# Moving the diagonal blocks of a chunked delta rule inside SBUF instead of through DRAM

## Chip, cores and metric

The kernel runs on one core of a Trainium2 chip. The metric is device time of one execution in microseconds (us). Three runs of the kernel before gave 1262.1 us as the median (1261.81 to 1263.61).

## What is computed

One layer of a hybrid encoder on a sequence of 2048 rows of 1024 numbers, all in float32: an input projection, a windowed attention in 8 heads, a gated delta rule in 4 heads that is run forward and backward, and an output projection. The change lies in the delta rule. Cut to that:

```python
def gated_delta_rule_chunked(q, k, v, g, beta):          # chunks of 64 in the reference
    ...
    k_beta = k * beta[..., None]
    m = jnp.where(strict, jnp.einsum('bhncd,bhnsd->bhncs', k_beta, k) * decay, 0.0)
    t_inv = lax.linalg.triangular_solve(eye + m, jnp.broadcast_to(eye, m.shape),
                                        left_side=True, lower=True, unit_diagonal=True)
    u = jnp.einsum('bhncs,bhnse->bhnce', t_inv, v * beta[..., None])
    w = jnp.einsum('bhncs,bhnsd->bhncd', t_inv, k_beta * jnp.exp(g)[..., None])
    ...
    def step(state, inp):                                # one chunk after another
        v_new = u_i - w_i @ state
        o = (q_i * exp(g_i)) @ state + a_i @ v_new
        state = state * exp(g_last) + k_dec.T @ v_new
```

So each chunk of each head and direction needs the inverse of a unit triangular matrix, and then the chunks of a head are scanned in order.

## The kernel before

**Stages.** `phase_a` makes the projections, the convolutions and the attention. `phase_b` does the delta rule head by head (h = 0 to 3), with chunks of 128 rows (16 chunks, in four groups `c4` of four), and then the output projection. For each head there are four stages:

- `pre_front(h)` loads keys, queries and values from DRAM, transposes them on TensorE, forms the products `gh`, and multiplies them on VectorE (DVE) with decay and beta into the matrices `ma` (L711): for each direction `d` and group `c4` a tile of 128 partitions x 4 chunks x 2 x 128.
- `solve(h)` inverts the diagonal 32x32 blocks: 2 directions x 16 chunks x 4 quarters = 128 blocks, one per partition, in tiles `L` (matrix) and `X` (inverse) of 128 x 32 x 32. It is a loop of 31 steps of two DVE instructions each (L749 multiplies into `tm`, L753 subtracts from `X`).
- `invert(h)` builds the inverses of the whole 128x128 matrices from the small ones, group by group (`hi`), with five products `pi` on TensorE; the small inverses are laid into the block-diagonal tiles `iv` (L776, on DVE and GpSimd (POOL)) and into `ma` (L793, POOL).
- `scan(h)` walks the 16 chunks in both directions at once: per step `pk` -> `r` (DVE) -> `py` -> `yk` (ScalarE, ACT) -> `po` -> state `S` (DVE).

**The path of the blocks.** A block that lies on 32 partitions of `ma` has to come onto one partition for the solve. Before, this goes through DRAM. L716 writes each `ma` matrix whole (256 KB) into `m_d`, whose rows are padded so that the diagonal blocks lie at a regular stride; L739 and L740 read the blocks back, for one direction into `X` and for the other into `L`; L742 copies `X` transposed into the lower half of `L` on DVE; then GpSimd clears `X` and sets its diagonal (L743, L744). After the last step L754 writes `X` to `x_d`, and `invert` reads eight pieces `xc` back (L765), which DVE turns in 32x32 blocks into `xt` (L766). All these DMAs are issued by SyncE (SP), whose queue is in order.

**Filling work.** `sw_units` has 32 units of the output projection for the attention half (`pcs`, L596 to L598 on TensorE, with `mhs` on ACT, `mls` L591 and `xrs` L599 on DVE, and the loads of `mxs` and `xrs` and the store of `part` on SP). They have no part in the delta rule and stand between its instructions.

**What sets the order.** The program's text does not. `set_order` builds the graph of dependences of all instructions, gives each a cost, plans the five engines forward and backward in turn, and pins the order on each engine (PE, DVE, ACT, POOL, SP) that came out best. A change in one place therefore moves instructions on all engines. Each engine works strictly in that order: an instruction that waits holds up all that stand behind it on its engine. `front(h+1)` and `solve(h+1)` run beside `scan(h)`; `invert(h+1)` follows `solve(h+1)`, and `scan(h+1)` follows `invert(h+1)`.

Of the kernel before, what the change touches and what calls it, by code (L numbers as in the profile page):

```python
# [7 lines left out]
F32 = mybir.dt.float32  # L8
F32R = mybir.dt.float32r
AF = mybir.ActivationFunctionType  # L10
# [5 lines left out]
P = 128  # L16
# [3 lines left out]
NCH = 16  # L20
# [526 lines left out]
def phase_b(ctx, wide, xe, ae, late, tc, t, ident, consts, hp, mix_dn, mix_sw, kq_d, v_d, zdn_d, zsw_d, dp, out):  # L547
    nc = tc.nc
    V, A, G, T = nc.vector, nc.scalar, nc.gpsimd, nc.tensor
# [91 lines left out]
    def pre_front(h):  # L641
# [7 lines left out]
        vs = H["vs"] = {}  # L649
        mp = {}  # L650
        ma = H["ma"] = {}
        m_d = dp.tile([2, NCH, 4 * (32 * P + 32)], F32, tag="m_d", name=f"m_d{h}", bufs=2)
        x_d = dp.tile([2, NCH, P, 32], F32, tag="x_d", name=f"x_d{h}", bufs=2)
        for n, c4 in enumerate(FRONT):
            s4 = slice(4 * c4, 4 * c4 + 4)
            cs = slice(c4 * 512, (c4 + 1) * 512)
# [34 lines left out]
            V.tensor_scalar(ssk[:, s4], ssk[:, s4], EPS, None, ALU.add)  # L691
            G.tensor_tensor(nk[:, s4], ssk[:, s4], pw[:, 0, :4], ALU.pow)  # L692
# [34 lines left out]
        for d in range(2):  # L727
            V.tensor_tensor(ck[:, d], bp[:, d], ekd[:, d, :, h], ALU.mult)

        H["solve"] = m_d, x_d, mp  # L730
        return H

    def solve(h, H):
        m_d, x_d, _ = H["solve"]
        L = qa.tile([P, 32, 32], F32, tag="L", name=f"L{h}")
        X = qa.tile([P, 32, 32], F32, tag="X", name=f"X{h}")
        lv = [m_d[d].rearrange("u (p y) -> (u p) y", p=4)[:, : 32 * P] for d in range(2)]
        lv = [a.rearrange("q (r x) -> q r x", x=P)[:, :, :32] for a in lv]
        dma(X[0:64], lv[0])  # L739
        dma(L[64:128], lv[1])  # L740
        x = X.rearrange("p r c -> p (r c)")
        V.tensor_copy(L[0:64], X[0:64].rearrange("p r c -> p c r"))  # L742
        G.memset(x, 0.0)  # L743
        G.memset(x[:, ::33], 1.0)  # L744
        for c in range(31):
            n = 31 - c
            tm = qa.tile([P, 256], F32, tag="tm", name=f"tm{h}_{c}")
            tv = tm[:, : n * (c + 1)].rearrange("p (r k) -> p r k", k=c + 1)
            V.tensor_tensor(  # L749
                tv, L[:, c + 1 :, c : c + 1].to_broadcast([P, n, c + 1]),  # L750
                X[:, c : c + 1, 0 : c + 1].to_broadcast([P, n, c + 1]), ALU.mult,
            )
            V.tensor_tensor(X[:, c + 1 :, 0 : c + 1], X[:, c + 1 :, 0 : c + 1], tv, ALU.subtract)  # L753
        dma(x_d.rearrange("d u (p r) c -> (d u p) (r c)", p=4), X.rearrange("p r c -> p (r c)"))  # L754

    def invert(h, H):
        _, x_d, mp = H["solve"]
        for hi in range(4):
            e1, p2, e2, e3 = (z[hi % len(z)] for z in zts)
            m = mp[hi]  # L760
# [1 line left out]
            for d, c4 in ((0, hi), (1, 3 - hi)):  # L762
                xc = qb.tile([P, 4, 32], F32, tag="xc", name=f"xc{h}_{d}_{c4}", bufs=4)
                xt = qb.tile([P, 4, 32], F32, tag="xt", name=f"xt{h}_{d}_{c4}", bufs=4)
                dma(xc, x_d[d, 4 * c4 : 4 * c4 + 4].rearrange("u i c -> i u c"))  # L765
                V.transpose(xt.rearrange("p u c -> p (u c)"), xc.rearrange("p u c -> p (u c)"))  # L766
# [97 lines left out]
    def post(h, H, groups):  # L864
        def of(a):
            return a.rearrange("p (g c) -> p g c", c=4)[:, groups[0] : groups[1] + 1 : groups[1] - groups[0]]

        nm = f"{h}_{groups[0]}"
        so = rp.tile([P, 2, 8], F32, tag="so", name=f"sso{nm}")
        for k, c4 in enumerate(groups):  # L870
            for c in range(4):
                jk = rp.tile([P, P], F32, tag="jko", name=f"jko{nm}_{k}_{c}", bufs=3)
# [544 lines left out]
```

## Time and profile before

| | |
|---|---|
| median of three runs | 1262.1 us (1261.81 to 1263.61) |
| the profiled execution, its time | 1270.01 us |
| its span in the profile | 1268.0 us |
| mean granted TensorE clock | 0.989 |
| DVE busy | 953.7 us (75% of the span) |
| ACT busy | 725.8 us (57%) |
| POOL busy | 529.2 us (42%) |

Busy time of an engine is the union of its instructions. A matmul's end is modelled, and matmuls overlap, so TensorE (PE) can be called busy without being at its peak. An idle time is put down to what released the instruction behind it; "<-" reads "was released by". In windows, each engine's busy time in a stretch is followed by its number of instructions; PEclk is the share of TensorE's clock that was granted, DMA the mean busy share of the 16 DMA engines. Rows of DMA issues give the time from issue to landing. In the time of the span, `phase_a` fills about the first 680 us, the delta rule's stages the stretch from there to about 1185, and the output projection of the delta half the rest.

### The profile page before, as it was taken

What the parts mean: (1) busy time and instruction counts of PE and PEld (TensorE: products, weight loads), DVE (VectorE), ACT (ScalarE), POOL (GpSimd) and SP (SyncE); (2) the same over time, 40 slices, a digit from 0 to 9 for tenths busy, and PEclk for the clock granted to TensorE, in tenths of its full rate; (3) what the DMA queues carried; (4) which work ended last, traced back from release to release, by engine and by line L of the source; (5) the groups of instructions that cost most, each with busy time, mean ns of one, the idle gap of its engine ahead of it and who ended that gap; (6) DMA issues with size and microseconds to landing.
All of it is one profiled execution on the core that took longest, in us unless ns stands there. A gap on an engine that the chain in (4) does not pass through costs nothing.

```text
span 1268.0 us, 22351 instructions
## 1 busy us (share of the span) xinstructions
PE 1210.5 (95%) x7018; PEld 1037.4 (82%) x7018; DVE 953.7 (75%) x2320; ACT 725.8 (57%) x2167; POOL 529.2 (42%) x845
## 2 busy tenths in 40 slices
PE   6999999999999999999999998999889899999898
PEld 5998888788889988887777777888789689888776
DVE  4523689999854379999995587698769779876765
ACT  6432476666534367766665438658557845685421
POOL 2243454763302276556422304613742441670541
PEclk9999999999999999999999999999889999999999
DMA  7553243513544434431016848967955875854785
GB/s 259 172 160 125 75 154 100 173 60 102 166 145 125 144 110 137 137 96 55 34 51 207 238 141 245 264 189 207 268 166 174 236 200 152 242 175 122 238 269 199
DMA packets 232294, 206.39 MB, mean 163 GB/s; under 512 B 49137, under 2 KB 181873, under 8 KB 232177
## 3 DMA queue, kind: packets, MB, share of 16 engines
q1 hardware_dynamic: 232176, 204.97, 53.0%
q8 instruction: 56, 0.92, 0.3%
q14 instruction: 62, 0.50, 0.1%
HBM read 139.84 MB, written 65.08 MB: 162 GB/s over the span
## 4 chain that ended last, share of the span: by engine, by line
PE 67%; DVE 13%; DMA 9%; ACT 4%; issue 3%; POOL 1%; SPq 1%; DVEq 0%; ACTq 0%; POOLq 0%
PE pf_c L199 5%; PE pf_c L201 5%; PE pf_c L200 5%; PE pf_z L199 4%; PE pf_z L200 4%; PE pf_z L201 4%; PE pi L781 3%; PE pq_q L212 2%; PE pq_q L211 2%; PE pt L390 2%; PE pq_q L210 2%; DMA xc<-x_d 2%; PE py L830 2%; PE po L839 2%; PE pcs L596 2%
## 5 line engine op out<-in xcount | busy, mean ns | idle before, releaser
L199 PE MATMUL pf_c<-xhi,wh_c 128*128 128x512 f32 x384 | 155.7, 405 | 0.8 <-DVE acc L269 0.8
L200 PE MATMUL pf_c<-xlo,wh_c 128*128 128x512 f32 x384 | 154.7, 403 | 0.0
L201 PE MATMUL pf_c<-xhi,wl_c 128*128 128x512 f32 x384 | 154.3, 402 | 0.0
L269 DVE SCALAR_TENSOR_TENSOR acc<-pf_c,cw,acc 128x512 f32<-128x512 f32 (+1 forms) x192 | 140.8, 742 | 2.6 <-POOL acc L259 0.7
L385 POOL TENSOR_SCALAR pr<-pr,st 128x384 f32<-128x384 f32 (+1 forms) x128 | 79.4, 639 | 98.0 <-DVE st L383 71.2
L394 ACT ACTIVATE ph<-pt 128x512 fp32r<-128x512 f32 x92 | 53.0, 595 | 60.5 <-PE pt L390 51.5
L376 ACT ACTIVATE pr<-pr,st 128x384 f32<-128x384 f32 (+1 forms) x128 | 76.2, 597 | 17.8 <-DVE st L372 17.4
L199 PEld LDWEIGHTS pf_c<-xhi,wh_c 128*128 128x128 f32 x384 | 72.5, 189 | 13.5 <-DVE acc L269 1.3
L201 PEld LDWEIGHTS pf_c<-xhi,wl_c 128*128 128x128 f32 x384 | 72.3, 188 | 12.9
L200 PEld LDWEIGHTS pf_c<-xlo,wh_c 128*128 128x128 f32 x384 | 72.4, 188 | 11.6
L835 ACT ACTIVATE yk<-py,ck 128x128 f32<-128x128 f32 x120 | 43.9, 366 | 62.0 <-PE py L830 61.2
L372 DVE CUSTOM_DVE_ANT_0 pr<-s,mask,sink 128x384 f32<-128x384 f32 (+1 forms) x128 | 73.4, 593 | 2.5 <-PE s L371 1.0
L211 PE MATMUL pq_q<-wh_q,xlo 128*128 128x256 f32 x256 | 72.1, 282 | 0.0
L212 PE MATMUL pq_q<-wl_q,xhi 128*128 128x256 f32 x256 | 71.9, 281 | 0.0
L210 PE MATMUL pq_q<-wh_q,xhi 128*128 128x256 f32 x256 | 71.4, 280 | 0.0
L390 PE MATMUL pt<-ident,pr 128*128 128x128 f32 x368 | 69.5, 274 | 1.8 <-DVE pl L395 1.1
L395 DVE TENSOR_TENSOR pl<-pt,ph 128x512 fp32r<-128x512 f32 x92 | 61.6, 681 | 6.1 <-ACT ph L394 5.6
L390 PEld LDWEIGHTS pt<-ident,pr 128*128 128x128 f32 x368 | 47.8, 140 | 20.4 <-DVE pl L395 4.4
L596 PE MATMUL pcs<-wohs,mhs 128*128 128x512 f32 x128 | 58.3, 456 | 4.4 <-ACT mhs L590 2.7
L692 POOL TENSOR_TENSOR nk<-ssk,pw 128x4 f32<-128x4 f32 x16 | 16.5, 1029 | 106.8 <-DVE ssk L691 106.6
L597 PE MATMUL pcs<-wohs,mls 128*128 128x512 f32 x128 | 56.1, 438 | 1.7 <-DVE mls L591 1.7
L598 PE MATMUL pcs<-wols,mhs 128*128 128x512 f32 x128 | 55.0, 429 | 0.0
(324 smaller groups left out, 4029.4 us busy)
## 6 DMA issues: line engine op xcount, KB each, us to landing
kqc<-kq_d SPq DMA_DIRECT2D x120, 128.0 KB, 3.1
ws_c<-wt SPq DMA_DIRECT2D x48, 256.0 KB, 3.5
xr<-x SPq DMA_DIRECT2D x16, 512.0 KB, 5.3
k_q<-kq_d SPq DMA_DIRECT2D x16, 512.0 KB, 5.6
mxs<-mix_sw SPq DMA_DIRECT2D x32, 256.0 KB, 3.7
xrs<-x SPq DMA_DIRECT2D x32, 256.0 KB, 3.7
part<-xrs SPq DMA_DIRECT2D x32, 256.0 KB, 2.6
xrd<-part SPq DMA_DIRECT2D x32, 256.0 KB, 4.1
```

Of the source, the lines that this page charges most:

```text
L199: T.matmul(ps, hi[:, k, cs], xhi[b][:, k], start=(k == 0), stop=False)
L200: T.matmul(ps, hi[:, k, cs], xlo[b][:, k], start=False, stop=False)
L201: T.matmul(ps, lo[:, k, cs], xhi[b][:, k], start=False, stop=(k == KC - 1))
L210: T.matmul(ps[:, :n], xh, hi[:, k, :n], start=(k == 0), stop=False)
L211: T.matmul(ps[:, :n], xl, hi[:, k, :n], start=False, stop=False)
L212: T.matmul(ps[:, :n], xh, lo[:, k, :n], start=False, stop=(k == KC - 1))
L269: V.scalar_tensor_tensor(av, ps[:, lo:], cw[:, i, k : k + 1], av, ALU.mult, ALU.add)
L372: V.tensor_tensor_reduce(pr[j][:, :n], ps[:, :n], mask[:, lo * P : hi * P], 1.0, sink[:, hh : hh + 1], ALU.add, ALU.min, accum_out=nm[:, j ...
L376: A.activation(pr[j][:, :n], pr[j][:, :n], AF.Exp, bias=nm[:, j : j + 1], scale=-1.0, accum_out=den[:, j : j + 1])
L385: G.tensor_scalar(pr[j][:, :n], pr[j][:, :n], den[:, j : j + 1], 1.0, ALU.mult, ALU.mult)
L390: T.transpose(pt[:, j], pr[j][:, (kb - lo) * P : (kb - lo + 1) * P], ident)
L596: T.matmul(ps, mh[:, k], wh[:, k], start=(k == 0), stop=False)
```

## The change

The blocks no longer leave SBUF. A tile `z` (128 partitions x 8 x 4 x 32) takes the place of `m_d`: each direction and half of the groups owns 32 partitions of it, and for each `ma` matrix four copies, one for each quarter, bring the diagonal blocks there, two on ACT and two on DVE. In `solve`, two 32x32 turns on DVE (64 partitions x 1024 each) make `L` from `z`; the scratch `tm` of the steps now lies in `z`. After the steps, one turn of 128 x 1024 makes `Y` from `X`, in the buffer of `L`. In `invert`, four copies (two on ACT, two on DVE) bring each piece from `Y` to `xt`, and the 32x32 turn, which was there before, now goes from `xt` to `xc`. To make room, the junk outputs `jk` and `jko` of the squares on ACT have one buffer in place of three, and a reserve of 1024 bytes per partition becomes 512.

```diff
-SCRATCH = 1024
+SCRATCH = 512
...
-        m_d = dp.tile([2, NCH, 4 * (32 * P + 32)], F32, tag="m_d", name=f"m_d{h}", bufs=2)
-        x_d = dp.tile([2, NCH, P, 32], F32, tag="x_d", name=f"x_d{h}", bufs=2)
+        z = qa.tile([P, 8, 4, 32], F32, tag="Z", name=f"Z{h}")
...
-                    jk = q1.tile([P, P], F32, tag="jk", name=f"jk{h}_{c4}_{j}_{c}", bufs=3)
+                    jk = q1.tile([P, P], F32, tag="jk", name=f"jk{h}_{c4}_{j}_{c}", bufs=1)
...
             for d in range(2):
-                dma(m_d[d, s4, : P * P].rearrange("u (i j) -> i u j", j=P), ma[d, c4][:, :, 0])
+                b = 32 * (2 * d + c4 // 2)
+                for p, q in enumerate(quads):
+                    a = z[b : b + 32, 4 * (c4 % 2) : 4 * (c4 % 2) + 4, p]
+                    if "VAVA"[p] == "A":
+                        A.activation(a, ma[d, c4][q, :, 0, q], AF.Copy)
+                    else:
+                        V.tensor_copy(a, ma[d, c4][q, :, 0, q])
...
     def solve(h, H):
-        m_d, x_d, _ = H["solve"]
+        z = H["solve"][0].rearrange("p u q j -> p j (u q)")
...
-        dma(X[0:64], lv[0])
-        dma(L[64:128], lv[1])
         x = X.rearrange("p r c -> p (r c)")
-        V.tensor_copy(L[0:64], X[0:64].rearrange("p r c -> p c r"))
         G.memset(x, 0.0)
         G.memset(x[:, ::33], 1.0)
+        V.transpose(L[0:64], z[0:64])
+        V.transpose(L[64:128].rearrange("p a b -> p b a"), z[64:128])
+        tm = H["solve"][0].rearrange("p u q j -> p (u q j)")[:, :256]
         for c in range(31):
...
-        dma(x_d.rearrange("d u (p r) c -> (d u p) (r c)", p=4), X.rearrange("p r c -> p (r c)"))
+        Y = H["Y"] = qa.tile([P, 8, 4, 32], F32, tag="L", name=f"Y{h}")
+        V.transpose(Y.rearrange("p u q r -> p r (u q)"), X)
...
-                dma(xc, x_d[d, 4 * c4 : 4 * c4 + 4].rearrange("u i c -> i u c"))
-                V.transpose(xt.rearrange("p u c -> p (u c)"), xc.rearrange("p u c -> p (u c)"))
+                b = 32 * (2 * d + c4 // 2)
+                for p, q in enumerate(quads):
+                    a = Y[b : b + 32, 4 * (c4 % 2) : 4 * (c4 % 2) + 4, p]
+                    if "VAVA"[p] == "A":
+                        A.activation(xt[q], a, AF.Copy)
+                    else:
+                        V.tensor_copy(xt[q], a)
+                V.transpose(xc.rearrange("p u c -> p (u c)"), xt.rearrange("p u c -> p (u c)"))
```

Because the planner sees new instructions, the order moves on every engine. Two places on DVE matter for the prediction. A row is line, operation, output<-inputs with the program's names, and shape; line numbers behind the change are shifted by up to nine.

The first place is where the solve of head 1 begins, beside the scan of head 0 (`r0_0_4` is step 4 of direction 0 of head 0). Before:

```order
L823 SCALAR_TENSOR_TENSOR r0_1_3_9197<-pk0_1_3_9195,negc_4920,vs0_3_8017 128x128
L591 TENSOR_TENSOR mls2_0_10138<-mxs2_0_10135,mhs2_0_10137 128x512
L842 SCALAR_TENSOR_TENSOR S0_0_3_9188<-S0_0_2_9148,egt_4922,po0_0_3_9180 128x128
L856 TENSOR_TENSOR oacc0_3_9091<-po0_1_2_9160,oacc0_3_9091 128x128
L742 COPY L1_10275<-X1_10276 64x1024
L823 SCALAR_TENSOR_TENSOR r0_0_4_9217<-pk0_0_4_9215,negc_4920,vs0_1_7827 128x128
L856 TENSOR_TENSOR oacc0_0_9078<-po0_0_3_9180,oacc0_0_9078 128x128
L842 SCALAR_TENSOR_TENSOR S0_1_3_9208<-S0_1_2_9168,egt_4922,po0_1_3_9200 128x128
L823 SCALAR_TENSOR_TENSOR r0_1_4_9238<-pk0_1_4_9236,negc_4920,vs0_2_7890 128x128
L749 TENSOR_TENSOR tm1_0_10282<-L1_10275,X1_10276 128x31
```

With the change:

```order
L851 SCALAR_TENSOR_TENSOR S0_1_1_9144<-S0_1_0_9104,egt_4922,po0_1_1_9136 128x128
L832 SCALAR_TENSOR_TENSOR r0_0_2_9153<-pk0_0_2_9151,negc_4920,vs0_0_7971 128x128
L865 TENSOR_TENSOR oacc0_0_9094<-po0_0_1_9116,oacc0_0_9094 128x128
L745 STREAM_TRANSPOSE L1_10314<-Z1_9798 64x1024
L775 STREAM_TRANSPOSE xc0_1_1_8926<-xt0_1_1_8927 128x128
L746 STREAM_TRANSPOSE L1_10314<-Z1_9798 64x32x32
L865 TENSOR_TENSOR oacc0_3_9107<-po0_1_1_9136,oacc0_3_9107 128x128
L751 TENSOR_TENSOR Z1_9798<-L1_10314,X1_10315 128x31
```

The first step of the solve has moved from behind step 4 of the scan to behind its step 2, and two turns stand where one copy stood.

The second place is where the same solve ends. Before (the last step is the row with `tm1_30` on its right):

```order
L749 TENSOR_TENSOR tm1_30_10372<-L1_10275,X1_10276 128x31
L694 TENSOR_TENSOR bp2_11356<-beta_4894,ssk2_11354 128x2x4
L842 SCALAR_TENSOR_TENSOR S0_0_14_9676<-S0_0_13_9636,egt_4922,po0_0_14_9668 128x128
L753 TENSOR_TENSOR X1_10276<-X1_10276,tm1_30_10372 128x31
L711 SCALAR_TENSOR_TENSOR ma2_0_11512<-gh2_0_0_11548,bp2_11356,v2_q_7736 128x2x128
L823 SCALAR_TENSOR_TENSOR r0_0_15_9705<-pk0_0_15_9703,negc_4920,vs0_3_8017 128x128
```

With the change:

```order
L755 TENSOR_TENSOR X1_10315<-X1_10315,Z1_9798 128x31
L710 SCALAR_TENSOR_TENSOR ma2_2_11399<-gh2_1_1_11443,bp2_11388,v2_q_7736 128x2x128
L851 SCALAR_TENSOR_TENSOR S0_0_11_9526<-S0_0_10_9486,egt_4922,po0_0_11_9518 128x128
L710 SCALAR_TENSOR_TENSOR ma2_1_11396<-gh2_1_1_11443,bp2_11388,v2_q_7736 128x2x128
L710 SCALAR_TENSOR_TENSOR ma2_2_11399<-gh2_1_1_11443,bp2_11388,v2_q_7736 128x2x128
L721 COPY Z2_11391<-ma2_1_11396 32x4x32
L832 SCALAR_TENSOR_TENSOR r0_0_12_9555<-pk0_0_12_9553,negc_4920,vs0_3_8040 128x128
L867 SCALAR_TENSOR_TENSOR oacc0_2_9268<-po0_0_11_9518,egc_4924,oacc0_2_9268 128x128
L757 STREAM_TRANSPOSE Y1_10382<-X1_10315 128x32x32
L868 TENSOR_TENSOR oacc0_2_9268<-po0_0_11_9518,oacc0_2_9268 128x128
L721 COPY Z2_11391<-ma2_1_11396 32x4x32
L774 COPY xt1_0_0_10385<-Y1_10382 32x128
```

The solve's end has moved from just ahead of the scan's last step (15) to ahead of step 12, and the turn into `Y`, the copies into `xt` and the first copies into `z` for head 2 stand among the scan's steps.

More of the change, by code (lines that the diff above doesn't have):

```diff
@@ L728, in pre_front @@
             V.tensor_tensor(ck[:, d], bp[:, d], ekd[:, d, :, h], ALU.mult)
-        H["solve"] = m_d, x_d, mp
+        H["solve"] = z, mp
         return H
     def solve(h, H):
-        m_d, x_d, _ = H["solve"]
+        z = H["solve"][0].rearrange("p u q j -> p j (u q)")
         L = qa.tile([P, 32, 32], F32, tag="L", name=f"L{h}")
         X = qa.tile([P, 32, 32], F32, tag="X", name=f"X{h}")
-        lv = [m_d[d].rearrange("u (p y) -> (u p) y", p=4)[:, : 32 * P] for d in range(2)]
-        lv = [a.rearrange("q (r x) -> q r x", x=P)[:, :, :32] for a in lv]
-        dma(X[0:64], lv[0])
-        dma(L[64:128], lv[1])
         x = X.rearrange("p r c -> p (r c)")
-        V.tensor_copy(L[0:64], X[0:64].rearrange("p r c -> p c r"))
         G.memset(x, 0.0)
         G.memset(x[:, ::33], 1.0)
+        V.transpose(L[0:64], z[0:64])
+        V.transpose(L[64:128].rearrange("p a b -> p b a"), z[64:128])
+        tm = H["solve"][0].rearrange("p u q j -> p (u q j)")[:, :256]
         for c in range(31):
             n = 31 - c
-            tm = qa.tile([P, 256], F32, tag="tm", name=f"tm{h}_{c}")
             tv = tm[:, : n * (c + 1)].rearrange("p (r k) -> p r k", k=c + 1)
@@ L753, in solve @@
             V.tensor_tensor(X[:, c + 1 :, 0 : c + 1], X[:, c + 1 :, 0 : c + 1], tv, ALU.subtract)
-        dma(x_d.rearrange("d u (p r) c -> (d u p) (r c)", p=4), X.rearrange("p r c -> p (r c)"))
+        Y = H["Y"] = qa.tile([P, 8, 4, 32], F32, tag="L", name=f"Y{h}")
+        V.transpose(Y.rearrange("p u q r -> p r (u q)"), X)
     def invert(h, H):
-        _, x_d, mp = H["solve"]
+        Y, mp = H["Y"], H["solve"][1]
         for hi in range(4):
@@ L871, in post @@
             for c in range(4):
[L872 removed]
+                jk = rp.tile([P, P], F32, tag="jko", name=f"jko{nm}_{k}_{c}", bufs=1)
                 A.activation(jk, H["oacc"][c4][:, c], AF.Square, accum_out=so[:, 0, 4 * k + c : 4 * k + c + 1])
```

## The prediction

> **What bounds the kernel now.** I read the page first: how busy each engine is, and the granted clock.
>
> ```profile
> span 1268.0 us, 22351 instructions
> PE 1210.5 (95%) x7018; PEld 1037.4 (82%) x7018; DVE 953.7 (75%) x2320; ACT 725.8 (57%) x2167; POOL 529.2 (42%) x845
> ```
>
> TensorE is busy for all but 57 us, so a change that takes nothing from it can at best win what it idles, plus what it loses to a lowered clock. Where is that? The windows answer, cut at the stages (each solve runs between two hand-overs, from one head's matrices and inverses to the next scan):
>
> ```profile
> core 0: us, PE busy (x) PEld busy (x) DVE busy (x) ACT busy (x) POOL busy (x), PEclk, DMA share, GB/s
> 40.00:680.00 640.00, 635.80 (x3527) 539.85 (x3526) 494.83 (x1050) 361.95 (x857) 289.90 (x453) 1.00 0.37 116
> 768.00:1115.00 347.00, 317.98 (x2109) 282.53 (x2107) 281.11 (x860) 228.80 (x873) 153.58 (x272) 0.97 0.74 214
> 768.00:823.00 55.00, 48.88 (x306) 42.37 (x305) 38.15 (x105) 40.74 (x149) 34.25 (x67) 0.97 0.95 272
> 823.00:882.00 59.00, 56.53 (x394) 50.49 (x393) 53.04 (x177) 40.88 (x168) 14.22 (x14) 1.00 0.67 197
> 882.00:934.00 52.00, 42.03 (x266) 37.13 (x264) 36.59 (x105) 32.55 (x125) 29.22 (x55) 0.93 0.87 241
> 934.00:990.00 56.00, 55.47 (x380) 50.71 (x381) 50.44 (x161) 38.82 (x157) 19.38 (x27) 0.95 0.59 179
> 990.00:1034.00 44.00, 37.09 (x225) 31.32 (x223) 31.72 (x95) 27.33 (x110) 22.77 (x50) 0.96 0.83 228
> 1034.00:1077.00 43.00, 42.37 (x294) 39.06 (x294) 39.01 (x129) 22.47 (x72) 7.97 (x18) 0.96 0.50 151
> 1077.00:1115.00 38.00, 35.62 (x253) 31.44 (x251) 32.16 (x94) 26.00 (x97) 25.76 (x43) 1.00 0.77 223
> ```
>
> The projections and the attention (40 to 680) leave TensorE idle for 4.2 us in 640: nothing to win there, however the planner shuffles them. The stretch 768 to 1115 has 29.0 us idle, of which the four hand-overs hold 25.4 (6.1, 10.0, 6.9, 2.4). The clock falls there too, and just behind: 1.7 us of full clock are lost in the first hand-over (0.03 of 55), then 3.6, 2.8, 1.8 and 1.7 in the next four rows. In the three solve windows (823, 934, 1034) TensorE is full and DVE is at 142.5 of 158 us, 90%. In the hand-overs DMA is at 0.77 to 0.95, and DVE idles for 50.4 us.
>
> What ends last in a hand-over? The chain of waits between 882 and 934, the waits of the same stretch, and the DMA queue's timeline:
>
> ```profile
> 882.43 6.82 DMA x_d<-X
> 889.27 4.05 DMA xc<-x_d
> ...
> 896.11 2.06 PE pi L781 x8
> ...
> 924.46 6.88 DMA xrs<-x
> 931.41 0.69 DVE xrs L599
> ```
>
> ```profile
> DVE xrs L599 <- DMA xrs<-x: 4.2, 1, 4.2
> PE pi L781 <- DVE iv L776: 3.6, 1, 3.6
> ```
>
> ```profile
> 914.49 3.90 SPq L740 DMA_DIRECT2D L<-m_d  x1
> 918.45 2.28 SPq L819 DMA_DIRECT2D kqc<-kq_d  x2
> ...
> 924.46 0.38 SPq L593 DMA_DIRECT2D xrs<-x  x1
> ```
>
> Two things are to be seen. After the solve, `x_d` and `xc` take 10.9 us before the first product `pi`, and TensorE waits 3.6 us for what they bring. And the issue of `L` holds SyncE's queue for 3.9 us; the queue is in order, so `xrs` of the filling unit is issued at 924.5 and lands at 931.3; DVE stands 4.2 us at L599 with the scan's state update behind it, and TensorE behind that:
>
> ```profile
> PE pk L821 <- DVE S L842: 3.8, 4, 3.2
> L740 SPq DMA_DIRECT2D L<-m_d x4: 597/3568/4602, 726.1 to 1021.9; - x4
> ```
>
> **The change, part by part.** Removed per head: eight writes `m_d`, `X`, `L`, `x_d`, eight reads `xc` (19 DMAs, 76 in all, from SyncE's queue), and the copy L742.
>
> ```profile
> m_d<-ma SPq DMA_DIRECT2D x20, 256.0 KB, 5.6
> x_d<-X SPq DMA_DIRECT2D x4, 512.0 KB, 6.4
> xc<-x_d SPq DMA_DIRECT2D x32, 64.0 KB, 4.0
> L<-m_d SPq DMA_DIRECT2D x4, 256.0 KB, 6.9
> L742 DVE COPY L<-X x4: 1096/1114/1120, 729.8 to 1026.6; 64x1024 f32<-64x1024 f32 x4
> ```
>
> That is 5.6 + 6.9 + 1.1 = 13.6 us of latency ahead of a solve and 6.4 + 4.0 = 10.4 behind it. Not all of it costs time, since the order puts a scan and filling work beside it. What it does cost, by the rows above: the 3.6 us of `pi`, the 3.8 of `pk`, and the lowered clock from 882 to 1077, which follows those idle times (3.6 + 2.8 + 1.8 + 1.7 = 9.9). I add 2 for the other hand-overs, where DVE also waits for `xc` (8.3 us in all, by the row of `xt` waits below). **Waits removed: 19 us.** Bounds: 7.4 if only the two waits go, 37 if all idle and all lost clock of the hand-overs go (25.4 + 11.6).
>
> Added per head on DVE: 16 copies into `z`, 16 into `xt`, two turns of 64x1024 and one of 128x1024. The nearest rows:
>
> ```profile
> L776 DVE COPY iv<-xc x48: 171/218/1206, 779.7 to 1110.2; 32x128 f32<-32x128 f32 x48
> L776 DVE COPY iv<-xt x48: 216/235/1303, 782.7 to 1110.6; 32x128 f32<-32x128 f32 x48
> L776 DVE COPY iv<-xt 32x128 f32<-32x128 f32 x48 | 15.6, 328 | 1.0
> L766 DVE STREAM_TRANSPOSE xt<-xc 128x128 f32<-128x128 f32 x32 | 9.4, 303 | 8.7 <-DMA xc<-x_d 8.3
> ```
>
> A copy of 32x128 takes 0.17 to 0.33 us (the least, and a mean that includes those held to 1.3); I take 0.25, near the medians. A turn of 1024 a partition is not in the trace. From below it costs what L742 does, 1.1 us; from above eight turns of 128, 2.4. I take 1.3, because the turn of 128 at 0.30 is near a plain DVE instruction of that size and a copy's 1.1 grows from there by little. So 32 x 0.25 + 3 x 1.3 - 1.1 = 10.8 us a head (bounds 7.7 and 16.7). [...]
>
> Between 768 and 1115 lie three heads' `z` copies and turns into `L` (3 x (4.0 + 1.5)) and four heads' `Y` and `xt` (4 x (1.3 + 4.0)): 37.7 us. DVE then has 281.1 + 37.7 = 318.8 us of work in that stretch, as much as TensorE (318.0 busy). **Here lies the price**: were the 19 us to go whole, the stretch would be 328 us and DVE 97% busy. It does reach that, but for 20 us at a time:
>
> ```profile
> 960.00:980.00 20.00, 20.00 (x150) 18.62 (x148) 19.60 (x65) 15.32 (x69) 3.82 (x3) 1.00 0.53 161
> 1040.00:1060.00 20.00, 20.00 (x148) 18.66 (x147) 19.35 (x62) 11.34 (x35) 0.00 (x0) 1.00 0.51 157
> ```
>
> Over a whole solve it is 90%, with TensorE as the bound. I take the middle of 90 and 97, 93.5%: 318.8 / 0.935 = 341 us for the stretch. **So DVE gives back 13 of the 19.**
>
> Added on ACT: 32 copies a head.
>
> ```profile
> L799 ACT ACTIVATE ma<-pi x40: 249/268/270, 790.5 to 1149.9; 32x128 f32<-32x128 f32 x40
> ```
>
> At 0.268 that is 8.6 us a head, 34 in all. ACT is idle in the hand-overs for 62 us of 189, which hides it; without that cover it costs what it takes. Before 768 head 0's copies and turns (5.5 us on DVE) lie beside the last gates, where TensorE is full: nothing. One buffer for `jk` and `jko` makes each square wait for its forerunner's end on ACT itself; the planner puts other ACT work between, and I cost it at nothing, with 34 us of the idle taken and 28 left as cover. `z` has one buffer and holds the solve's scratch: copies for head 2 cannot start before the solve of head 1 has ended, and on DVE the rest of `ma` would be late behind them; the order shows the first such copy five rows behind the solve's last step, so this too is nothing. TensorE gets no instruction.
>
> **The sum.** -19 + 13 = -6 us. In the profiled execution that is 1270.0 to 1264 (span 1268 to 1262); it was 7.9 us above the median, so against the median 1262.1 the forecast is **1256 us**. A difference under 0.2%, 2.5 us, cannot be told from no change.
>
> **Rivals.** (1) *DVE becomes the bound, and the kernel slower.* The place is the same stretch. If DVE stays at the 90% of the solve windows, it needs 318.8 / 0.90 = 354 us, 7 more than now: 1269 us; with the upper prices of copy and turn (16.7 a head, some 57 us in the stretch) 376, or 1291. It decides from 92% on: 318.8 / 347. For it speaks that the copies stand in front of scan steps in the order (the second place); against it that the 90% are what TensorE, full there, leaves to DVE. (2) *The waits go and DVE finds room*: 97%, the full 19 us: 1243 us. For it: 50.4 us of DVE idle in the hand-overs, and the solve ends earlier, at step 12 of the scan. (3) *The transfers were hidden anyway*: the scan's chain ends the hand-over, other loads (`xrs`, `kqc`) still land late, and what was won in one queue is waited for in the next: 1262 us. For it: the waits of TensorE in a hand-over are many and short, with other names. [...] Of the same copy some take 1.2 to 1.3 us against a median of 0.22, while GpSimd copies beside them stretch too:
>
> ```profile
> L776 POOL COPY iv<-xt x48: 281/292/808, 789.7 to 1133.8; 32x128 f32<-32x128 f32 x48
> ```
>
> If every added copy is charged the mean, 0.32, the 112 copies of the stretch are 8 us more work: 327 / 0.935 = 349, or 1264 us. [...]
>
> **Chances.** Forecast (1251 to 1262 us) 0.42; rival 1 0.28; rival 2 0.16; rival 3 0.09; rival 4 0.05. Faster by over 0.2%: 0.33 of the forecast, rival 2, and 0.01 of rival 3, in all 0.50. Within 0.2%: 0.07 + 0.01 + 0.06 + 0.02 = 0.16. Slower: 0.02 + 0.27 + 0.02 + 0.03 = 0.34. The range, 1238 to 1276, takes in rival 2 with half its spread (a gain of 24) and rival 1 with half the way to its upper prices; about 0.18 lies outside. The forecast's own range is 1251 (DVE at 95%) to 1262 (92%).
>
> **What would show it.** Right: no wait for `xc`, no issue of 3 us and more on SyncE in the hand-overs, `pi` of head 1 following the solve's last step by some 5 us (a turn, two copies, a turn) and not 14; PEclk above 0.97 from 882 on; DVE over 92% busy between the first inverse and the last. The turn's row gives its price, the copies' rows theirs. Wrong: a span of the stretch over 347 us with DVE above 90% (rival 1), DVE idle in the hand-overs as now (rival 3), or copies with a mean over 0.3 (rival 4).

## The result and the profile after

| | before | after |
|---|---|---|
| median of three runs | 1262.1 us | 1300.08 us (1296.17 to 1300.3) |
| the profiled execution, its span | 1268.0 us | 1298.5 us |
| mean granted TensorE clock | 0.989 | 0.989 |

The kernel became slower by 38 us: the ratio is 1.0288, with a 95% interval of 1.0256 to 1.032. The prediction was 1256 us with a range up to 1276; both the sign and the range were wrong. The two profiled spans lie 30.5 us apart, so the profiles below account for that much of the loss.

The page of the kernel after, engines and three lines of the 40 slices:

```profile
PE 1218.4 (94%) x7018; PEld 1037.0 (80%) x7018; DVE 1021.8 (79%) x2456; ACT 778.9 (60%) x2295; POOL 535.2 (41%) x845
DVE  4523689999754289999985789899999999976775
ACT  5432466755633367666666756768957875786421
DMA  7554242522552444322015736555656444663785
```

TensorE has the same 7018 products. DVE is busy 68 us longer, ACT 53, and DMA is no longer high between slices 24 and 36. Where did TensorE lose the time? The windows of the kernel before, cut at 680, at the end of the first solve and at the end of the last (columns as in the prediction):

```profile
0.00:680.00 680.00, 664.42 (x3711) 566.66 (x3712) 511.47 (x1079) 384.64 (x906) 301.72 (x485) 1.00 0.39 126
680.00:768.00 88.00, 85.25 (x403) 68.83 (x402) 58.18 (x162) 43.32 (x171) 14.09 (x13) 1.00 0.63 179
768.00:1077.00 309.00, 282.37 (x1859) 251.09 (x1857) 248.95 (x766) 202.80 (x777) 127.82 (x229) 0.96 0.74 212
1077.00:1268.00 191.00, 178.42 (x1052) 150.81 (x1050) 135.12 (x314) 95.01 (x316) 85.52 (x118) 1.00 0.67 207
```

The same four stages after, then the three hand-overs (last step of one solve to first step of the next), and at last the stretch of which the prediction spoke, from the first inverse on:

```profile
0.00:680.00 680.00, 659.28 (x3673) 561.53 (x3674) 504.94 (x1045) 376.52 (x878) 302.22 (x479) 1.00 0.39 122
680.00:788.00 108.00, 101.93 (x485) 81.60 (x484) 79.96 (x220) 67.12 (x233) 19.26 (x21) 0.98 0.56 161
788.00:1100.00 312.00, 274.44 (x1801) 240.63 (x1800) 291.63 (x862) 233.16 (x853) 125.18 (x226) 0.97 0.54 166
1100.00:1298.50 198.50, 182.79 (x1065) 153.20 (x1063) 145.25 (x332) 102.14 (x332) 88.56 (x119) 1.00 0.63 199
...
788.00:838.00 50.00, 36.27 (x207) 29.61 (x205) 43.74 (x111) 41.78 (x145) 27.05 (x54) 0.90 0.61 190
890.00:945.00 55.00, 44.96 (x282) 37.27 (x280) 53.03 (x155) 50.90 (x198) 26.46 (x46) 1.00 0.62 192
992.00:1059.00 67.00, 57.92 (x359) 49.54 (x357) 62.68 (x183) 57.82 (x226) 25.67 (x49) 0.95 0.51 156
...
788.00:1137.00 349.00, 307.39 (x2033) 269.53 (x2032) 326.29 (x964) 260.42 (x947) 147.72 (x270) 0.97 0.55 167
```

TensorE's idle time is a window's length less its busy time. Up to the end of the first solve it went from 18.3 to 26.8 us, between the first solve and the last from 26.6 to 37.6, and behind it from 12.6 to 15.7: 22.6 us more in all; the other 7.9 us of the span lie in TensorE's busy time, and why the same products keep it busy longer is not shown. Of the idle time, 5.1 us came up before 680 (15.6 to 20.7), where no added instruction has run yet: there only the order has changed. In the three hand-overs DVE is now busy for 159.5 of 172 us (93%) and ACT for 150.5 (88%). Before, there was room: DVE idled for 50.4 us of the four.

The wait of 3.6 us that TensorE had for `iv` is gone. Others took its place; four of the longest from 788 to 1137 (us in all, times, longest):

```profile
PE gh L701 <- DVE xhi_h L710: 4.6, 2, 2.9
PE py L839 <- DVE r L832: 3.4, 7, 0.8
PE tr L681 <- ACT ks L684: 3.3, 1, 3.3
PE po L841 <- DVE zt L899: 2.8, 2, 2.2
```

All rows of this view added up, DVE ended 24.9 us of TensorE's waits and ACT 13.0; in the same view of before (768 to 1115) it was 17.5 and 9.1.

DVE's timeline behind the solve of head 1 shows what took the place of the transfers (start, us, line, operation; before, the chain had `x_d` and `xc` here, 10.9 us):

```profile
890.71 0.17 DVE L755 TENSOR_TENSOR X<-X,Z 128x31 f32<-128x31 f32 x1
890.80 0.47 DVE L710 SCALAR_TENSOR_TENSOR ma<-gh,bp,v_q 128x256 f32<-128x256 f32 x1
891.20 0.33 DVE L851 SCALAR_TENSOR_TENSOR S<-S,egt,po 128x128 f32<-128x128 f32 x1
891.46 0.86 DVE L710 SCALAR_TENSOR_TENSOR ma<-gh,bp,v_q 128x256 f32<-128x256 f32 x2
...
892.89 1.95 DVE L757 STREAM_TRANSPOSE Y<-X 128x1024 f32<-128x1024 f32 x1
...
895.00 0.93 DVE L721 COPY Z<-ma 32x128 f32<-32x128 f32 x1
895.96 0.22 DVE L774 COPY xt<-Y 32x128 f32<-32x128 f32 x1
...
897.19 0.22 DVE L774 COPY xt<-Y 32x128 f32<-32x128 f32 x1
...
899.59 1.06 DVE L774 COPY xt<-Y 32x128 f32<-32x128 f32 x1
...
901.00 0.88 DVE L774 COPY xt<-Y 32x128 f32<-32x128 f32 x1
```

The first row is the solve's last step. Between it, `Y` and the copies into `xt` stand products for the `ma` of the next head, the scan's `r`, `S` and `oacc`, and copies into `z`; DVE goes from one to the next without a rest, and two of the four `xt` copies take 1.06 and 0.88 us. POOL's timeline has these two rows (the second is two instructions):

```profile
894.91 0.95 POOL L743 MEMSET X<- 128x1024 f32 x1 [5.15 <-DVE Y L757]
899.30 2.49 POOL L672 TENSOR_TENSOR v_q<-v_q,dmask 128x512 f32<-128x512 f32 x2
```

The three long copies each run beside one of these instructions and end less than 0.1 us behind it. It is so in the whole trace: 15 of the 128 added DVE copies took over 0.4 us, and every one of them ended 0.07 to 0.09 us behind an instruction of POOL beside it, while the median copy took 0.22. Such long copies are what the fourth rival charged, with every added copy at the mean of 0.32 us (1264 us); what the 15 took above the median comes to 12 us of DVE over the four heads. That POOL's instructions hold them is not shown: 46 of the other 113 copies also had one beside them, and no run takes POOL's work away.

PE's timeline has the first `pi` of this inverse at 911.17 us, 20.3 us behind the end of the last step; before it was 14.1 (882.0 to 896.11). TensorE did not idle for it this time; the planner had put other products ahead of it:

```profile
911.17 0.39 PE L790 MATMUL pi<-iv,g 128*128 128x128 f32 x2
```

The new rows among the groups by line (busy us, mean ns):

```profile
L774 DVE COPY xt<-Y 32x128 f32<-32x128 f32 x64 | 21.3, 332 | 1.4
L772 ACT ACTIVATE xt<-Y 32x128 f32<-32x128 f32 x64 | 19.7, 307 | 2.3 <-DVE Y L757 1.0
L721 DVE COPY Z<-ma 32x128 f32<-32x128 f32 x40 | 11.8, 295 | 0.7
L746 DVE STREAM_TRANSPOSE L<-Z 64x1024 f32<-64x1024 f32 x4 | 8.4, 2105 | 0.1
L745 DVE STREAM_TRANSPOSE L<-Z 64x1024 f32<-64x1024 f32 x4 | 8.1, 2032 | 0.0
L757 DVE STREAM_TRANSPOSE Y<-X 128x1024 f32<-128x1024 f32 x4 | 7.9, 1967 | 0.0
```

### The profile page after: what moved, and what is told of

It reads as the page before. It is cut to its first block, busy times and chain, and to the rows that moved or that the text cites. A ratio compares the mean times of both kernels' runs of the same rounds, so it can differ in the third digit from the quotient of the medians.

```text
span 1298.5 us, 22500 instructions
## 1 busy us (share of the span) xinstructions
PE 1218.4 (94%) x7018; PEld 1037.0 (80%) x7018; DVE 1021.8 (79%) x2456; ACT 778.9 (60%) x2295; POOL 535.2 (41%) x845
## 4 chain that ended last, share of the span: by engine, by line
PE 58%; DVE 19%; ACT 8%; DMA 7%; issue 4%; POOL 3%; SPq 1%; DVEq 0%; POOLq 0%; ACTq 0%
PE pf_c L201 4%; PE pf_c L200 4%; PE pf_c L199 4%; PE pf_z L199 3%; PE pf_z L201 3%; PE pf_z L200 3%; DVE acc L269 3%; PE pi L790 3%; PE pq_q L212 2%; PE pq_q L211 2%; PE pq_q L210 2%; DMA zs<-wt 2%; PE pt L390 2%; PE py L839 2%; PE po L848 2%
## 5 line engine op out<-in xcount | busy, mean ns | idle before, releaser
L691 POOL TENSOR_TENSOR nk<-ssk,pw 128x4 f32<-128x4 f32 x16 | 16.7, 1045 | 109.3 <-DVE ssk L690 104.1
L190 ACT ACTIVATE wh_c<-ws_c 128x512 fp32r<-128x512 f32 x48 | 30.2, 629 | 50.4 <-DMA ws_c<-wt 20.3
L596 PE MATMUL pcs<-wohs,mhs 128*128 128x512 f32 x128 | 55.7, 435 | 1.8 <-ACT mhs L590 0.6
```

## The experiments

Eighteen kernels were run. Times are medians, ratios are to runs of the kernel before on the same chip (its median lay between 1261.4 and 1264.7 us). They ask four things: what is the order worth by itself, what the single junk buffer, what the copies, what the planner's price of a turn.

### What a new order costs, with nothing else changed

The kernel before, with one constant of the planner moved. Not one instruction differs, only the order.

```diff
-LAG = {"PE": 205, "DVE": 140, "Activation": 160, "Pool": 120, "SP": 2400}
+LAG = {"PE": 205, "DVE": 140, "Activation": 160, "Pool": 120, "SP": 2390}   # e5_nudge_sp
+LAG = {"PE": 206, "DVE": 140, "Activation": 160, "Pool": 120, "SP": 2400}   # e6_nudge_pe
+LAG = {"PE": 205, "DVE": 141, "Activation": 160, "Pool": 120, "SP": 2400}   # e18_nudge_dve
```

> The kernel before, with one of the planner's constants nudged (the lag of a DMA 2390 in place of 2400 ns): same instructions, another order. Theory D (the kernel before stands on an order that came out well, and any edit that makes the planner plan anew loses 10 to 20 us): 1270 to 1285 us. Theory C (the junk buffer's own waits cost what e1 lost): 1262 us within 4.

> The kernel before, with another constant nudged (the lag of TensorE 206 in place of 205 ns): a second draw of the order. Theory D: 1270 to 1285 us, not the same as e5. Theory C: 1262 us within 4.

> The kernel before with the lag that the planner reckons for DVE at 141 in place of 140 ns; no instruction added or removed. Two such nudges gave 1270.9 and 1274.7 us, and the order planned for one junk buffer 1282.6 with the buffers unchanged. Theory A (the order of the kernel before is a chosen one, and any other plan loses 7 to 20 us): 1268 to 1283 us. Theory B (the losses of the earlier plans are chance, as many draws lie at or below 1262): 1255 to 1265 us.

Measured: 1270.89 us, ratio 1.0056 (1.0032 to 1.008); 1274.74, 1.0085 (1.0065 to 1.0105); 1274.46, 1.0105 (1.0064 to 1.0145). All three lose, by 7 to 13 us (their ratios, of 1262). A fourth order of the same instructions, e13 below, loses 20. So the order of the kernel before is a good one among those that the planner draws, and each of the four other draws gave that up. Against the three nudged ones the change lost some 25 to 30 us, against e13 18, not 38.

### The single junk buffer

In the kernel before: one buffer for `jk` and `jko` (and the reserve of 512 bytes); the same with the planner told that there are three, so that the order stays that of before; and the reverse, three buffers with the planner told that there is one. In the changed kernel: three buffers, in bf16 so that they fit.

```diff
-  jk = q1.tile([P, P], F32, tag="jk", ..., bufs=3)     # and jko
+  jk = q1.tile([P, P], F32, tag="jk", ..., bufs=1)     # e1, e7
...
+  bufs = 3 if tag.startswith("jk") else m.bufs         # in set_order: e7
+  bufs = 1 if tag.startswith("jk") else m.bufs         # in set_order: e13, with bufs=3 above
...
-  jk = q1.tile([P, P], F32, tag="jk", ..., bufs=1)     # after
+  jk = q1.tile([P, P], mybir.dt.bfloat16, tag="jk", ..., bufs=3)   # e8
```

> The kernel before, with the junk tiles jk and jko in one buffer and the reserve of 512 bytes; the blocks still go through DRAM. Theory A (the added DVE work is what costs): nothing of it is here, 1262 us, within 3. Theory B (the planner prices the turns and copies too low and leaves too little slack): also 1262, give or take what another order does, some 3 us. Theory C (the single junk buffer makes the squares on ACT wait for each other and draws out the front stage): 1275 to 1295 us, with longer fronts, most of the loss.

> The kernel before with jk and jko in one buffer, while the planner is told three: the order on every engine is that of the kernel before, so only the waits between the squares on ACT are new. Theory C: 1275 to 1285 us, as e1 (1282). Theory D: 1262 to 1266, and the 20 us of e1 come from the order.

> The kernel before with its three junk buffers, but with the planner told that there is one (and 512 bytes more room), so that the order is that of the kernel with one junk buffer (1282.2 us), without the waits for a single buffer. Theory A (waits and order add: 8 us of waits by the run that kept the old order, 10 to 12 of order as in the two nudged plans): 1271 to 1276 us. Theory B (the waits are all of it, the order is free): 1262 to 1265. Theory C (the order is all of it): 1280 to 1283.

> The changed kernel with three buffers for jk and jko again, in bfloat16 so that they fit (the junk is never read). Theory C: 20 of the 38 us come back, 1280 us or lower. Theory D: another draw of the order, anything from 1280 to 1305. Theory A: 1300 as the changed kernel.

Measured: e1 1282.17 us, ratio 1.0163 (1.0139 to 1.0187); e7 1272.69, 1.0061 (1.004 to 1.0081); e13 1282.55, 1.0163 (1.014 to 1.0186); e8 1291.73, 1.022 (1.0191 to 1.0248).

e7 is the clean run: the order is kept, and the single buffer costs 8 us, between what Theory C and Theory D had. The page shows how; it is of the longest execution, 1281.4 us, where the other four took 1272.0 to 1272.7. Its row of engines:

```profile
PE 1214.7 (95%) x7018; PEld 1038.9 (81%) x7018; DVE 956.9 (75%) x2320; ACT 741.4 (58%) x2167; POOL 532.1 (42%) x845
```

ACT is busy for 741.4 us with the same 2167 instructions, against 725.8. The durations of ACT's instructions, added up, are the same (871.8 and 871.2 us); what has grown is their union. With three buffers 175 of the 192 squares begin before the instruction ahead of them on ACT has ended, with one 34 do: 15.6 us, 0.08 us for each square. The waits of DVE from 680 to 1185 show it arriving, first before, then in e7:

```profile
DVE ssk L691 <- ACT jk L690: 8.6, 6, 4.9
DVE ma L711 <- ACT jko L873: 0.9, 1, 0.9
```

```profile
DVE ssk L691 <- ACT jk L690: 12.2, 9, 5.8
DVE ma L711 <- ACT jko L873: 2.2, 1, 2.2
DVE sso L876 <- ACT jko L873: 1.7, 3, 0.8
```

e13 corrects this for another order: with the order that the planner draws for one buffer, three buffers and one take the same time (1282.6 and 1282.2), so there the waits cost nothing and the order all of the 20 us (ACT is busy for 736.9 us in e1 and 729.3 in e13, a growth of half the size). Theory C of e13 held, and the sum "waits and order" that e1 had suggested fell. In the changed kernel, three buffers gain 8 us (1300.1 to 1291.7, intervals apart), though with a new order too; the 20 us of Theory C of e8 did not come.

### Each half alone

e2 is the change with `x_d` and `xc` as before, so only the way from the matrices to the solve lies in SBUF (with one junk buffer). e3 is the kernel before with only the way from the solve to the inverse in SBUF (three junk buffers).

```diff
+  dma(x_d.rearrange("d u (p r) c -> (d u p) (r c)", p=4), X.rearrange("p r c -> p (r c)"))   # e2, in place of Y
+  dma(xc, x_d[d, 4 * c4 : 4 * c4 + 4].rearrange("u i c -> i u c"))                             # e2, in place of the xt copies
...
+  V.transpose(Y.rearrange("p u q r -> p r (u q)"), X)                                          # e3, in place of x_d; xt copies as in the change
```

> The changed kernel, but only the matrices go to the solve inside SBUF; from the solve to the inverse the blocks go through DRAM as before. Of the 68 us that DVE is longer busy with the change, the copies into z and the turns into L less the removed copy are 32, the rest 29. Theory A: loss in proportion, 38 x 32 / 68 = 18, so 1280 us. Theory B: the two turns of 2.05 us that the planner takes for 1.13 are on the path to the solve here, 1275 to 1285. Theory C: the junk buffer is here, so 1285 to 1300.

> The kernel before, but the solve's result goes to the inverse inside SBUF (one turn, copies into xt); the matrices go to the solve through DRAM; junk tiles with three buffers. DVE gets 29 of the 68 us. Theory A: 38 x 29 / 68 = 16, so 1278 us. Theory B: one underpriced turn a head, 1265 to 1275. Theory C: no loss, or the gain of the removed x_d and xc waits, 1250 to 1262.

Measured: 1278.68 us, ratio 1.0139 (1.0119 to 1.0159); 1274.72, 1.0107 (1.008 to 1.0135). The second half alone takes as long as a nudged plan of the kernel before: beyond the lost order nothing is seen of it. The first half alone lies 4 to 8 us over those draws, about what its single junk buffer can cost. The two losses, 16 and 12 us, do not reach 38: both halves together cost more than their sum. That would follow if both fill the same engines; with a new order in each run it is not shown.

### The copies

In the change: all copies on ACT (e4). In e8, the change with three junk buffers: DVE's half on POOL (e9), every copy as a DMA from SBUF to SBUF (e11), every copy twice (e14), one copy of four (e16; three quarters of `z` and `xt` are cleared on POOL in their place, so those diagonal blocks are left out of what is computed).

```diff
-  if "VAVA"[p] == "A":
+  if "AAAA"[p] == "A":                          # e4
...
-  V.tensor_copy(a, ma[d, c4][q, :, 0, q])       # and V.tensor_copy(xt[q], a)
+  G.tensor_copy(a, ma[d, c4][q, :, 0, q])       # e9
...
+  dma(a, ma[d, c4][q, :, 0, q])                 # e11, for all four, and dma(xt[q], a)
...
   V.tensor_copy(a, ma[d, c4][q, :, 0, q])
+  V.tensor_copy(a, ma[d, c4][q, :, 0, q])       # e14, the same for ACT's and for xt
...
+  if p == 0:                                    # e16
       V.tensor_copy(xt[q], a)
+  else:
+      G.memset(xt[q], 0.0)
```

> The changed kernel with all copies on ACT (32 a head more there, some 39 us in all) and none on DVE (41 us less); the turns stay. Theory A: DVE is left with 27 of the 68 us, so 1262 + 38 x 27 / 68 = 1277 us or lower, unless ACT becomes the bound. Theory B: the turns are still underpriced, 1290 to 1300. Theory C: ACT is loaded further, 1300 or more.

> As e8 (three junk buffers), with the copies that were on DVE on GpSimd: 41 us less on DVE, about 37 more on POOL, ACT as in e8. Theory E (in the hand-overs DVE and ACT are both filled by the copies and turns, DVE 93 to 95%, ACT 85 to 89%, so that shifting work between them, as e4 did, wins nothing): DVE falls to some 80% there and the time to 1275 to 1283 us. Theory B (underpriced turns): 1288 to 1295, as e8. Theory D alone (order luck): no direction, 1280 to 1300.

> As e8, with all 64 copies a head made by DMA from SBUF to SBUF, so that DVE and ACT have only the turns to do more than in the kernel before (24 us less 4 for the copy that went). One DMA leg stands where two were, and the matrices are not written out whole. Theory E: the hand-overs are free of the copies, 1265 to 1278 us, the level of the nudged kernels (1271 and 1275) or better. Theory B: 1285 to 1295, the turns are as before. If it is the wait for DMAs that set the hand-overs, also better than e8 only in part, 1280 to 1290.

> The change with three junk buffers (1291.7 us), each copy between quarters made twice (128 more on DVE, 128 more on ACT; the second writes the same as the first, so the result is the same). Theory A (DVE and ACT are full in the hand-overs, so an added copy costs its time there): about 128 x 0.32 = 41 us more on DVE, of which three quarters lie in the stretch of the hand-overs: 15 to 35 us slower, 1307 to 1327 us. Theory B (the copies fit into idle time and the loss is of the order alone): within 8 us, 1284 to 1300 us.

> The change with three junk buffers (1291.7 us) with one copy of four left: of each matrix and of each piece only the first quarter is copied, on DVE; the other quarters of z and xt are cleared on POOL instead, so three of four diagonal blocks are left out of what is computed, while the turns, the solve and all products stay. It takes 128 copies from ACT and 64 from DVE. Theory A (an added copy costs its time: 256 copies more cost 30 us when every one was made twice, so 192 fewer give back 20 to 25): 1265 to 1275 us. Theory B (the second set of copies cost because the first had used up the idle time; the first was mostly hidden): 1280 to 1292 us.

| | us | ratio (95%) | DVE, ACT in the three hand-overs | TensorE's idle in them |
|---|---|---|---|---|
| e4, all on ACT | 1297.81 | 1.0285 (1.0259 to 1.031) | 76%, 93% | 32.0 of 185 us |
| e8, as in the change | 1291.73 | 1.022 (1.0191 to 1.0248) | 94%, 87% | 32.5 of 163 |
| e9, DVE's on POOL | 1282.96 | 1.0159 (1.0108 to 1.021) | 85%, 86% | 25.4 of 146 |
| e11, by DMA | 1328.03 | 1.0518 (1.0477 to 1.056) | - | - |
| e14, twice | 1321.94 | 1.0474 (1.0455 to 1.0493) | 93%, 86% | 46.3 of 198 |
| e16, one of four | 1273.8 | 1.0098 (1.0064 to 1.0132) | 94%, 74% | 20.0 of 136 |

The hand-overs of e14 and of e16, from which two rows of the table come (the others the same way, each cut at its own solves):

```profile
788.00:845.00 57.00, 39.48 (x181) 29.83 (x180) 53.62 (x142) 47.46 (x164) 21.69 (x41) 0.85 0.56 180
891.00:965.00 74.00, 58.91 (x346) 48.57 (x345) 67.94 (x199) 64.23 (x250) 37.35 (x62) 0.93 0.54 169
1017.00:1084.00 67.00, 53.36 (x290) 42.63 (x291) 61.66 (x187) 57.63 (x218) 23.14 (x47) 0.92 0.45 139
```

```profile
778.00:820.00 42.00, 34.91 (x211) 28.72 (x210) 39.01 (x93) 28.36 (x102) 30.00 (x78) 1.00 0.72 224
875.00:921.00 46.00, 38.25 (x257) 32.95 (x256) 42.52 (x129) 34.77 (x150) 27.69 (x62) 1.00 0.66 190
981.00:1029.00 48.00, 42.82 (x272) 35.99 (x270) 46.29 (x137) 37.63 (x163) 28.93 (x66) 1.00 0.57 176
```

With the copies doubled the share of DVE and ACT stays where it was, and the hand-overs grow by 35 us: the engines were full, so an added copy costs most of its time. DVE is busy for 37.7 us more than in e8 and ACT for 41.4, and the kernel takes 30 us longer. It is the same from the other side: three of four copies less take 18.9 us from DVE and 38.1 from ACT, and give back 18 us. The 30 us stand clear of what a draw of the order cost anywhere here (20), the 18 only of the three nudges. Theory A of e14 held, and that of e16 (near the upper end of its range). Which engine makes the copies matters less: on ACT alone the fill moves from DVE (76%) to ACT (93%), and nothing is gained (Theory A of e4, 1277 us, failed); on POOL, which had the most idle time, DVE's half costs 9 us less, which a draw of the order can nearly explain by itself (6 us, e15 below).

The DMAs were the worst, beyond every theory of e11 (1265 to 1295 us). SyncE issues 256 of them, and each holds its queue for 0.6 us, 159 us in all; POOL and DVE wait for what they bring. The source view of the pieces `xt` in e11: SyncE's issues of them, and who waited for them (us, times):

```profile
L768 SPq DMA_DIRECT2D xt<-Y x128: 585/599/1612, 789.8 to 1185.0; - x128
...
  POOL iv L779: 26.6, 6
  DVE xc L769: 13.0, 7
```

### The planner's price of a turn, and both remedies together

The planner had priced a turn by the rule for other DVE instructions. e10 gives it the measured one; e12 adds e9's copies on POOL; e17 is e12 with SyncE's lag at 2390, and e15 is e8 with that lag.

```diff
+            if "ranspose" in str(i.opcode):
+                return 62 + 1.94 * m        # e10, e12, e17
...
+    G.tensor_copy(xt[q], a)                 # e12, e17, in place of V; z's copies too
...
-LAG = {... "SP": 2400}
+LAG = {... "SP": 2390}                      # e15, e17
```

> As e8, with the planner's price of a 32x32 turn set to what the profile shows (62 ns + 1.94 ns an element: 2.05 us for 1024 a partition in place of 1.14). Theory B: the planner leaves the room, 1272 to 1282 us. Theory E: the work is still there, 1287 to 1296. Theory D: anything within 8 of 1292.

> The change with three junk buffers, with DVE's half of the copies on POOL, and with the planner told the measured price of a turn (62 ns + 1.94 ns for each element of a partition). Alone, the first of these two brought 1291.7 to 1283.0, the second to 1284.2. Theory A (what is left over the kernel before is DVE's and ACT's fill, part of it ordered by a wrong price): the gains add in part, 1274 to 1279 us, and TensorE's stall in the hand-overs falls below the 42 us of the POOL version. Theory B (both gains are luck of the order and say nothing of copies and turns): the two don't add, 1280 to 1288 us.

> The change with three junk buffers and one constant of the planner moved (the lag that it reckons for SyncE, 2400 to 2390 ns), as in the nudge of the kernel before that cost 7 us. Theory A (the order of the changed kernel is one draw from a scatter of some us, and 1291.7 no unlucky one): 1285 to 1297 us. Theory B (the order of the changed kernel is an unlucky draw by itself, and most of the loss is that): one other draw falls to 1270 to 1280 us.

> The change with three junk buffers, DVE's half of the copies on POOL and the measured price of a turn in the planner (1279.3 us), with the planner's lag for SyncE at 2390 in place of 2400. Theory A (what is left over the kernel before is partly the scatter that any new plan shows, 3 to 8 us either way): 1272 to 1286 us, above 1262 either way. Theory B (the change made well is worth its 19 us of waits, and only the order hides it): a draw below 1262 us.

Measured: e10 1284.22 us, ratio 1.0173 (1.0132 to 1.0213), between Theory B and Theory E and inside Theory D; e12 1279.27, 1.0138 (1.0117 to 1.0159); e15 1285.34, 1.0195 (1.0165 to 1.0225); e17 1273.8, 1.0097 (1.0064 to 1.013). The two remedies add in part, 12 us of 16 (at the upper end of Theory A of e12), and one more draw takes 5.5 us away. e15 shows what a draw alone is worth in the changed kernel, 6 us; by that measure POOL alone (9 us) and the price alone (7.5) are not shown one by one. Both together gain 12.5 us at one lag (e8 to e12) and 11.5 at the other (e15 to e17), which two pairs of draws make likely.

The hand-overs of e17:

```profile
772.00:815.00 43.00, 33.19 (x193) 27.39 (x192) 34.16 (x80) 37.26 (x131) 30.18 (x79) 0.96 0.73 222
871.00:921.00 50.00, 42.91 (x278) 36.17 (x277) 41.99 (x114) 47.05 (x188) 35.16 (x78) 1.00 0.65 201
968.00:1028.00 60.00, 51.36 (x313) 43.15 (x313) 50.72 (x140) 51.54 (x209) 34.38 (x80) 0.97 0.56 173
```

DVE is at 83% there, and TensorE idles for 25.5 us in place of 32.9. So the best version of the change, at 1273.8 us, takes as long as the nudged plans of the kernel before (1270.9 to 1274.7). No version came below the kernel before.

## Why the prediction was wrong, step by step

**The sum that the runs give.** From the change back: three junk buffers 8 us (1300.1 to 1291.7), DVE's copies on POOL and the right price 12 (to 1279.3), another draw of the order 5.5 (to 1273.8), and 12 that are left over the kernel before, as much as a nudged plan of that kernel loses (7 to 13; e13 20). Each step draws a new order as well: two orders of the changed kernel lay 6 us apart, the four other ones of the kernel before 13, and no term holds to less. That the last 12 us are the lost order alone is likely by the nudges, not shown: no run gave the changed kernel the order of before.

**"So DVE gives back 13 of the 19"** is the step that failed. The price was right in kind and too small. A head's turns took 6.1 us (2.03 + 2.10 + 1.97) where 3.9 were taken: "the turn of 128 at 0.30 is near a plain DVE instruction" was the wrong one of the two bounds, since from 128 elements a partition (0.302 us) to 1024 (1.97 to 2.10) each one added 1.9 ns, and 1024 of them cost near the upper bound. The copies took 0.32 us on the mean, just what the fourth rival took, with the 15 of over 0.4 us in it; 0.25 was near the median, 0.22. A head then adds some 15 us on DVE, not 10.8; the upper bound was 16.7. With these prices the same step gives 334 us of work, 334 / 0.935 = 357 for the stretch and some 1273 us, so the price is some 17 of the 44 us by which the forecast was off. The rest is what the following paragraphs name: the waits that took the place of the removed ones, and two terms that the sum put at nothing, the single buffer and the new order.

**The 93.5% came true by luck and told nothing.** From 788 to 1137 DVE is busy for 326.3 of 349 us, just that share; but TensorE did 2033 products there and not 2109, since the planner had drawn other work ahead. The length of a stretch whose content moves cannot carry a sum; the idle time of TensorE over the whole span does. The first rival, DVE as the bound, came nearest to the hand-overs, and its sign came (349 us at 93%); but ACT is nearly as full there, and moving the copies from DVE to ACT gained nothing (e4). It, too, looked for the loss in this stretch alone (1269 us, at most 1291).

**"Waits removed: 19 us."** The transfers went as predicted: no DMA releases an idle DVE from 788 to 1137, where `xc` had cost 8.3 us, and the longest issue of SyncE from 760 to 1140 takes 1.4 us, where `L` had held the queue for up to 4.6. But the idle time didn't go with them: TensorE's waits for DVE and ACT in that stretch grew from 26.6 to 37.9 us. Nor did the clock come back: the first hand-over is at 0.90, and from the first solve to the last PEclk is 0.97 for 0.96; that it follows TensorE's idle time was an estimate and is not shown, since the idle time there was 37.6 us for 26.6. "`pi` of head 1 following the solve's last step by some 5 us" fell hardest, with 20.3 us: the turn and the copies on that path each stand in DVE's queue behind other work.

**"ACT is idle in the hand-overs for 62 us of 189, which hides it."** The idle time was there, but it was not cover. With the copies in it, ACT is at 88% and DVE at 93%, and the scan's chain goes through both at every step. Idle time between the links of this chain was its slack, not free room; e14 is the run for it: with every copy twice, the kernel took 30 us longer, DVE and ACT at 93% and 86% of the hand-overs (94% and 87% in e8).

**"I cost it at nothing"**, of the junk buffers: 8 us in the order of before (e7), nothing in another (e13).

**"Nothing to win there, however the planner shuffles them"**: nothing to win, but to lose. The first solve ends at 788 instead of 768 us. Up to there TensorE idles 8.5 us longer; the other 11.5 us are busy time, with 44 products drawn ahead (4158 by then, 4114 before). What stood behind the sentence, that a new plan is as good as the one it replaces, is what the three runs with one constant moved and e13 refute. Neither the forecast nor any rival had a term for it.

**Two slips in the working.** Half the way from 1269 to rival 1's upper 1291 is 1280, not the 1276 at which the range ends. And the rows with a lowered clock are not the next four: the one from 823 to 882 has 1.00. Neither would have changed the outcome.

## What to carry to other kernels

A transfer that ends last in the chain is not yet time to be won: ask what takes its place on the engines that the same stretch keeps busy, count the added instructions at the price of their slowest near kin (a mean with the long ones in it, 0.32 us here, not a median, 0.22), and take idle time on an engine of the chain for slack until a run shows that it hides work (double the suspected cost and halve it; both are cheap). Where a planner or a scheduler draws the order, first move one of its constants by a hair and see what any new order costs; here four orders cost 7 to 20 us, a fifth to half of the loss, before one instruction had changed. And a single buffer for an output that nobody reads can still make its writers wait for one another: in e7 that cost 8 us.

## What the runs showed of the hardware that was not expected

- A 32x32 turn on DVE in float32 took 0.302 us for 128 elements a partition and 1.97 to 2.10 us for 1024, some 1.9 ns for each element between; on 64 partitions it took 2.03 and 2.10 us, on 128 partitions 1.97.
- With three buffers for their outputs 175 of the 192 squares on ACT began before the instruction ahead of them had ended; with one buffer, in the same order, 34 did, and the same instructions kept ACT busy for 15.6 us more of the span (7.6 in another order, e1 over e13), while their durations added up to the same (871.8 and 871.2 us).
- A copy of 32x128 took nearly the same on DVE (0.32 us on the mean, 0.22 the median), ACT (0.31) and POOL (0.34 on the mean, 0.29 the median, its copies into `iv` in the kernel after).
- All 15 of the 128 added copies on DVE that took over 0.4 us ended 0.07 to 0.09 us behind an instruction of POOL beside them; 46 of the other 113 had one beside them too.
- Each of the 256 DMAs of 16 KB from SBUF to SBUF in e11 held SyncE's queue for 0.6 us at its issue (the median), longer than any of the three engines took for the copy on the mean.
